# Query blocks in the order 1 to 7, 0, later turns of results, and retention weights loaded two inner blocks at a time

## The chip, the cores and the metric

The kernel runs on one core of a Trainium2 chip. The metric is device time in microseconds (us), the median of the runs shown. The engines are TensorE (PE; its weight loads are PEld), VectorE (DVE), ScalarE (ACT), GpSimd (POOL) and SyncE (SP), which here only issues DMAs.

## The reference

One layer of a decoder with three parallel branches: retention, causal pooling, and a sparse attention (NSA). It runs over a prompt of 1024 tokens and over 8 samples of 8 tokens each, with model width 1024. What the change touches is the prompt's attention and the projections of retention:

```python
z = rms_norm(x, gain) @ w_in              # 1024 -> 8984 columns, split into q, k, v, gates of all branches
o_a, s = retention(rq, rk, rv, state)     # 4 heads, chunks of 128 tokens, a 128 x 256 state a head
# attention, 8 heads in 2 groups; for every query block of 128 tokens:
o_cmp = softmax(q kc + bias) vc           # 32 compressed rows (means of 32 tokens)
o_sel = softmax(q ks + bias) vs           # all earlier tokens (16 blocks of 64 are chosen, which is all of them)
o_win = softmax(q kw + bias) vw           # the last 512 tokens
o = g0 * o_cmp + g1 * o_sel + g2 * o_win  # sigmoid gates by head
b_c = (silu(ng) * o) @ w_br_c             # likewise b_a = (silu(rg) * o_a) @ w_br_a, and b_b for pooling
y = x + (g_a * b_a + g_b * b_b + g_c * b_c) @ w_out
```

Query block i (128 tokens) reads i + 1 key blocks in the selected branch and min(i + 1, 5) in the window branch. So block 0 has one key block in each branch, and block 7 has 8 and 5.

## The kernel before

Every operand is kept as two half-precision parts (hi and lo), and a product takes three matmuls. The stages follow one another: the projections of keys, values and queries (to about 150 us of the profile), the prompt's attention (to about 496), retention (to about 740), pooling and the samples' attention (to about 880), then branch and output products. The program is written with a tile framework: its compile-time scheduler orders the instructions of each engine by modelled times and priority (earlier code first), and that order is then fixed. `issue_after(x)` and `behind()` place instructions behind a given instruction of their own engine.

*Attention.* `prompt_attention` (L719) goes through 64 heads: query blocks `order` = 0 to 7, two groups g, four heads r each. It is a pipeline over n. Step n issues the scores of head n (`head_scores`, L847: matmuls L863, L875, L884; DVE adds the bias and finds the maximum, L869 and L895), then the values of head n - 3 (LAG = 3; `head_values`, L784, matmuls L1344 to L1346 through `mm3`), then the probabilities of head n - 1 (`head_probs`, L760). The probabilities of each branch are made on ACT (L772, L773) and split into hi and lo (DVE L777, POOL L778, tile `hl`), and both parts are turned by a DMA transpose that SP issues (L780, `pt` from `hl`). `hl` and `pt` have two buffers for each branch, the score tile `S` has four.

When the four heads of a group are done (r = 3), `head_norm` (L897) scales the values by gates and sums (L903, DVE) and adds the three branches (L905 and L906, POOL) in the tile `ob`, which has one buffer. `head_out` (L909), called one step later, at r = 1 of the next group as the values lag, turns the result on PE (L913, "to") and gates it. Once a block, at n % 8 == 3, `cmp_attention` makes the compressed branch; it and `head_out` share the single PSUM buffer "tr".

*Fill.* So that PE does not stand, steps are filled with matmuls of other projections (the generator `fill`: 192 units from `silu_c` for retention's gate, then 168 from `early_gates` for the branch gates; a unit is three matmuls L319 to L321 of up to 384 columns). A head of block i brings FILL_A * (i + 1 + min(i + 1, 5)) + FILL_B = 4.0 (block 0) to 6.2 (block 7) units. 336 units go with the heads, 6 after the last head, and the last 18 in any place behind the last scores (`self.after`). Ahead of the heads stand 96 units of `silu_c` for attention's own gate.

*Weights of retention.* `load_r` (L276) loads the columns of one retention head, 8 inner blocks k of 128 x 512. Each k takes a buffer `raw` of 128 x 1024 (half used), two DMAs of 128 KB (L284, L285) and a split into `rwh` and `rwl` (`wsplit`, L230: ACT L232, DVE L233). For head 0 ACT issues the DMAs and there are two raw buffers, which the fill's weights use as well (`load_c`); for the other heads SP issues them and there are three. The retention projections (`proj_t`, L289: L298 to L300, tile z) go through k in order.

On SP, between the last transposes of attention, stand retention's constants, above all two DMAs of 512 KB for the rotary tables (`rope`, L1158).

Of the kernel before, what the change touches and what calls it, by code (L numbers as in the profile page):

```python
# [16 lines left out]
ALU = mybir.AluOpType  # L17
# [3 lines left out]
P = 128  # L21
# [17 lines left out]
LAG = 3  # L39
# [22 lines left out]
C_RET = 0  # L62
# [65 lines left out]
class Kern:  # L128
# [147 lines left out]
    def load_r(self, pool, h):  # L276

        hi, lo = [pool.tile([P, 8, 512], F16, tag="rw" + x, name=self.nm("rw" + x), bufs=1) for x in "hl"]
        w = self.d["w_in"][0]
        for k in range(8):  # L280
            raw = self.wtile([P, 1024], F32, "raw")
            r = slice(k * P, k * P + P)
            qk = w[r, C_RET:C_RET + 1024].rearrange("p (a h c) -> p a h c", a=2, c=P)[:, :, h, :]
            self.wq.dma_start(raw[:, 0:256].rearrange("p (a c) -> p a c", c=P), qk)  # L284
            self.wq.dma_start(raw[:, 256:512], w[r, 1024 + h * 256:1280 + h * 256])  # L285
            self.wsplit(hi[:, k, :], lo[:, k, :], raw[:, :512])
        return hi, lo

    def proj_t(self, out, hi, lo, t, c0, n):  # L289
# [428 lines left out]

    def prompt_attention(self, sp, ps, fill):  # L719

        order = range(8)
        heads = [(i, g, r) for i in order for g in range(2) for r in range(4)]
        sc, pr, out, oc = {}, {}, None, {}
        quota = 0.0
        for n in range(64 + LAG):
            if n < 64:
                sc[n] = self.head_scores(*heads[n], sp, ps)
            if n >= LAG:
                i, g, r = heads[n - LAG]
                if r == 0:  # L730
                    self.o = ps.tile([P, 2, 4, 64], F32, tag="o", name=self.nm("o"), bufs=A_O)
                s, nm, l = sc.pop(n - LAG)
                self.head_values(i, g, r, s, pr.pop(n - LAG), self.o, sp, ps)
                if r == 1 and out:
                    self.head_out(*out, sp, ps)
                if r == 3:
                    out = (i, g, self.head_norm(i, g, self.o, l, oc[i], sp))
            if 1 <= n <= 64:
                i, g, r = heads[n - 1]
                pr[n - 1] = self.head_probs(i, r, sc[n - 1], sp)  # L740
            if n < 64:
                i = heads[n][0]
                quota += FILL_A * (i + 1 + min(i + 1, 5)) + FILL_B
                with self.tc.issue_after(self.after.ins):
                    while quota >= 1:
                        next(fill, None)
                        quota -= 1
                if n % 8 == 3:
                    oc[i] = self.cmp_attention(i, sp, ps)
        for _ in range(6):  # L750
            next(fill, None)
        with self.tc.issue_after(self.filled.ins):
            self.head_out(*out, sp, ps)
# [140 lines left out]
    def far(self, out, in_, cf, m_in, m_out):  # L894
        self.nc.vector.tensor_scalar(out, in_, cf, m_in, op0=ALU.add, op1=ALU.max, accum_out=m_out)  # L895

    def head_norm(self, i, g, o, l, oc, sp):  # L897
        nc = self.nc
        gt = self.gate[:, i, 8:24].rearrange("p (b h) -> p b h", h=8)[:, :, 4 * g:4 * g + 4]
        self.norm_gates(l[:, 2], l[:, 0], l[:, 1], gt)  # L900
        ob = sp.tile([P, 2, 4, 64], F32, tag="ob", name=self.nm("ob"), bufs=1)
        f = l[:, 2].rearrange("p b h -> p (b h)")[:, :, None].to_broadcast([P, 8, 64])
        nc.vector.tensor_tensor(ob.rearrange("p b h c -> p (b h) c"), o.rearrange("p b h c -> p (b h) c"), f,  # L903
                                op=ALU.mult)
        nc.gpsimd.tensor_tensor(ob[:, 0], ob[:, 0], oc[:, 4 * g:4 * g + 4, :], op=ALU.add)  # L905
        nc.gpsimd.tensor_tensor(ob[:, 0], ob[:, 0], ob[:, 1], op=ALU.add)  # L906
        return ob

    def head_out(self, i, g, ob, sp, ps):  # L909
# [1074 lines left out]
```

## Time and profile before

| | |
|---|---|
| median of 3 runs | 1303.39 us (1302.78 to 1307.32) |
| the profiled execution | 1306.33 us, span 1304.5 us |
| mean granted TensorE clock | 0.986 |
| PE busy | 1251.2 us (96%) |
| PE weight loads busy | 849.4 us (65%) |
| DVE busy | 912.6 us (70%) |
| ACT busy | 630.8 us (48%) |
| POOL busy | 524.8 us (40%) |

Busy time is time in which an instruction runs on the engine; a busy PE is not PE at its peak, since the ends of its pipelined matmuls are modelled. The granted clock is the mean share of full speed that the throttle let PE have.

### The profile page before, as it was taken

Reading aid. Unit: us, or ns where it says so; the run is one execution under the profiler, and the core shown is the slowest. Engines: PE = TensorE matmul, PEld = TensorE weight load, DVE = VectorE, ACT = ScalarE, POOL = GpSimd, SP = SyncE. Lnnn points to the kernel's source line nnn. Section 1 sums busy time; section 2 is a strip of 40 time slices with the busy share of each in tenths; the row PEclk is TensorE's granted clock in tenths of the full one; section 3 lists DMA queues with packets and bytes.
Section 4 is the critical chain, followed back from the end, with each engine's and each line's share of the span. In section 5 each row is a group of like instructions: output and inputs, shape, how many; then the busy total and the mean of one; then the engine's idle time right before and its main releaser. Section 6 shows DMA issues by size and latency. Waiting matters only on the chain. (4 is left out here: it accounts for less than half of the span.)

```text
span 1304.5 us, 27790 instructions
## 1 busy us (share of the span) xinstructions
PE 1251.2 (96%) x10520; PEld 849.4 (65%) x10520; DVE 912.6 (70%) x2288; ACT 630.8 (48%) x1474; POOL 524.8 (40%) x562
## 2 busy tenths in 40 slices
PE   7999999989999989999999999999999999999995
PEld 4555666767677765555555566657788888888452
DVE  6747635788777864776766568662798877578976
ACT  5623445676666763555654444433534333212332
POOL 1112114567666751445553550101743666322124
PEclk9999999999999999999999999998999999999998
DMA  7867724598999995243741378326542121543623
GB/s 260 184 124 152 166 57 91 96 151 152 150 174 206 188 216 157 78 108 104 189 125 28 87 224 246 86 83 233 178 130 66 50 59 48 186 143 108 218 68 127
DMA packets 323419, 179.24 MB, mean 137 GB/s; under 512 B 204433, under 2 KB 297585, under 8 KB 322868
## 3 DMA queue, kind: packets, MB, share of 16 engines
q1 hardware_dynamic: 282804, 137.27, 45.3%
q10 hardware_dynamic: 35600, 26.32, 6.8%
q0 software_dynamic: 4880, 13.87, 3.3%
q8 instruction: 82, 1.34, 0.4%
q14 instruction: 53, 0.43, 0.1%
HBM read 98.80 MB, written 33.25 MB: 101 GB/s over the span
## 5 line engine op out<-in xcount | busy, mean ns | idle before, releaser
L778 POOL TENSOR_TENSOR hl<-S,hl 128x640 f16<-128x640 f32 (+7 forms) x128 | 153.9, 1211 | 122.3 <-DVE hl L777 79.5
L319 PE MATMUL pj<-xh,whi 128*128 128x384 f16 (+1 forms) x480 | 152.2, 317 | 2.4 <-ACT ue L1439 1.1
L321 PE MATMUL pj<-xh,wlo 128*128 128x384 f16 (+1 forms) x480 | 152.2, 317 | 0.0
L320 PE MATMUL pj<-xl,whi 128*128 128x384 f16 (+1 forms) x480 | 152.2, 317 | 0.0
L298 PE MATMUL z<-rwh,xh 128*128 128x512 f16 x256 | 97.7, 382 | 0.0
L300 PE MATMUL z<-rwh,xl 128*128 128x512 f16 x256 | 97.5, 381 | 0.0
L299 PE MATMUL z<-rwl,xh 128*128 128x512 f16 x256 | 97.5, 381 | 0.0
L773 ACT ACTIVATE S<-S,nm 128x640 f32<-128x640 f32 (+7 forms) x128 | 93.7, 732 | 5.4 <-DVE hst L869 1.1
L321 PEld LDWEIGHTS <-wlo 128*128 128x128 f16 x672 | 66.0, 98 | 36.5 <-issue 1.0
L320 PEld LDWEIGHTS <-whi 128*128 128x128 f16 x672 | 66.1, 98 | 36.1 <-issue 4.9
L1588 DVE TENSOR_TENSOR q<-st,q 128x288 f32<-128x288 f32 (+1 forms) x168 | 70.2, 433 | 26.4 <-PE st L1579 25.4
L319 PEld LDWEIGHTS <-whi 128*128 128x128 f16 x672 | 66.0, 98 | 33.4 <-issue 1.2
L298 PEld LDWEIGHTS <-xh 128*128 128x128 f16 x448 | 45.2, 101 | 45.7 <-issue 6.1
L232 ACT ACTIVATE whi<-raw 128x1024 f16<-128x1024 f32 (+1 forms) x48 | 45.4, 947 | 60.1 <-PE pj L320 14.7
L300 PEld LDWEIGHTS <-xl 128*128 128x128 f16 x448 | 44.1, 98 | 46.1 <-issue 2.8
L299 PEld LDWEIGHTS <-xh 128*128 128x128 f16 x448 | 44.3, 99 | 45.8 <-issue 4.8
L1344 PE MATMUL o<-vst,pt 128*128 128x64 f16 x528 | 56.7, 194 | 11.6 <-DMA pt<-hl 11.3
L772 ACT ACTIVATE hl<-S,nm 128x128 f16<-128x128 f32 (+7 forms) x64 | 49.1, 767 | 37.1 <-DMA pt<-hl 37.1
L777 DVE CAST hl<-S 128x640 f16<-128x640 f32 (+4 forms) x64 | 31.9, 498 | 50.0 <-DMA pt<-hl 18.9
L1276 POOL TENSOR_TENSOR rh<-rot,rh 128x256 f16<-128x256 f32 (+1 forms) x36 | 25.9, 720 | 90.2 <-ACT rh L1275 89.8
L320 PE MATMUL eg<-xl,whi 128*128 128x384 f16 (+1 forms) x192 | 62.1, 323 | 0.0
L321 PE MATMUL eg<-xh,wlo 128*128 128x384 f16 (+1 forms) x192 | 62.1, 323 | 0.0
(516 smaller groups left out, 4056.5 us busy)
## 6 DMA issues: line engine op xcount, KB each, us to landing
raw<-w_in SPq DMA_DIRECT2D x26, 512.0 KB
raw<-w_in ACTq DMA_DIRECT2D x18, 512.0 KB
raw<-w_in SPq DMA_DIRECT2D x48, 128.0 KB
wad<-q ACTq DMA_DIRECT2D x21, 256.0 KB
raw<-egd SPq DMA_DIRECT2D x16, 272.0 KB
s<-state_ret SPq DMA_DIRECT2D x16, 256.0 KB
o_ret_s<-s POOLq DMA_DIRECT2D x16, 256.0 KB
wr<-w_out SPq DMA_DIRECT2D x8, 512.0 KB
```

Source lines behind the costliest of these rows:

```text
L232: a = nc.scalar.activation(hi, raw, AF.Copy, scale=WS)
L298: nc.tensor.matmul(out, xh, hi[:, k, c0:c0 + n], start=(k == 0), stop=False)
L299: nc.tensor.matmul(out, xh, lo[:, k, c0:c0 + n], start=False, stop=False)
L300: self.marks["PE"] = nc.tensor.matmul(out, xl, hi[:, k, c0:c0 + n], start=False, stop=(k == 7))
L319: nc.tensor.matmul(out, hi[:, k, :], xh, start=(k == 0), stop=False)
L320: nc.tensor.matmul(out, hi[:, k, :], xl, start=False, stop=False)
L321: self.filled = nc.tensor.matmul(out, lo[:, k, :], xh, start=False, stop=(k == 7))
L772: nc.scalar.activation(hl[:, :w], s[:, d0:c1], AF.Exp, bias=nm[:, br:br + 1], scale=0.125)
L773: nc.scalar.activation(s[:, c0:c1], s[:, c0:c1], AF.Exp, bias=nm[:, br:br + 1], scale=0.125, accum_out=l[:, 0, br, r:r + 1])
L778: nc.gpsimd.tensor_tensor(hl[:, w:2 * w], s[:, d0:c1], hl[:, :w], op=ALU.subtract)
L1344: nc.tensor.matmul(out, lhs[0], rhs[0], start=start, stop=False)
L1588: nc.vector.tensor_tensor(out[:, c0:c0 + n], b, x[:, c0:c0 + n], op=ALU.add)
```

## The change

Four edits. The query blocks go in the order 1, 2, ..., 7, 0. `head_out` is called at r = 2 of the next group, one head later than before. The two additions of the very last group (n - LAG = 63) are made on DVE, all others on POOL as before. `load_r` puts two inner blocks into one `raw` buffer (four DMAs of 128 KB) and splits both with one instruction on each engine, 128 x 1024.

```diff
@@ load_r
-        for k in range(8):
+        for k2 in range(0, 8, 2):
             raw = self.wtile([P, 1024], F32, "raw")
-            r = slice(k * P, k * P + P)
-            qk = w[r, C_RET:C_RET + 1024].rearrange("p (a h c) -> p a h c", a=2, c=P)[:, :, h, :]
-            self.wq.dma_start(raw[:, 0:256].rearrange("p (a c) -> p a c", c=P), qk)
-            self.wq.dma_start(raw[:, 256:512], w[r, 1024 + h * 256:1280 + h * 256])
-            self.wsplit(hi[:, k, :], lo[:, k, :], raw[:, :512])
+            for i in range(2):
+                r = slice((k2 + i) * P, (k2 + i) * P + P)
+                qk = w[r, C_RET:C_RET + 1024].rearrange("p (a h c) -> p a h c", a=2, c=P)[:, :, h, :]
+                x = raw[:, 512 * i:512 * i + 512]
+                self.wq.dma_start(x[:, 0:256].rearrange("p (a c) -> p a c", c=P), qk)
+                self.wq.dma_start(x[:, 256:512], w[r, 1024 + h * 256:1280 + h * 256])
+            self.wsplit(*[x[:, k2:k2 + 2, :].rearrange("p k c -> p (k c)") for x in (hi, lo)], raw)
@@ prompt_attention
-        order = range(8)
+        nc = self.nc
+
+        order = (*range(1, 8), 0)
...
-                if r == 1 and out:
+                if r == 2 and out:
                     self.head_out(*out, sp, ps)
                 if r == 3:
-                    out = (i, g, self.head_norm(i, g, self.o, l, oc[i], sp))
+                    out = (i, g, self.head_norm(i, g, self.o, l, oc[i], sp, nc.vector if n - LAG == 63 else nc.gpsimd))
@@ head_norm
-    def head_norm(self, i, g, o, l, oc, sp):
+    def head_norm(self, i, g, o, l, oc, sp, eng):
...
-        nc.gpsimd.tensor_tensor(ob[:, 0], ob[:, 0], oc[:, 4 * g:4 * g + 4, :], op=ALU.add)
-        nc.gpsimd.tensor_tensor(ob[:, 0], ob[:, 0], ob[:, 1], op=ALU.add)
+        eng.tensor_tensor(ob[:, 0], ob[:, 0], oc[:, 4 * g:4 * g + 4, :], op=ALU.add)
+        eng.tensor_tensor(ob[:, 0], ob[:, 0], ob[:, 1], op=ALU.add)
```

## Rows read from the trace of the kernel before

**Rows 1.** Windows by stage: length, busy time by engine, granted clock, DMA share, GB/s.

```profile
205.00:470.00 265.00, 255.72 (x2989) 185.78 (x2987) 205.00 (x676) 184.67 (x413) 175.08 (x153) 0.99 0.89 157
470.00:497.00 27.00, 21.89 (x259) 15.08 (x258) 11.46 (x25) 12.11 (x22) 9.50 (x8) 0.94 1.05 235
```

**Rows 2.** PE's waits, 150 to 470 us: us in total, times, longest.

```profile
PE o L1344 <- DMA pt<-hl: 7.3, 11, 1.9
PE to L913 <- POOL ob L906: 1.7, 2, 1.0
```

**Rows 3.** Waits, 470 to 500 us.

```profile
PE o L1344 <- DMA pt<-hl: 4.0, 2, 3.8
```

**Rows 4.** Timeline of PE at the seam: start, us, instruction, [idle before <- releaser].

```profile
468.56 0.60 PE L863 MATMUL pn<-kst,qst 128*128 128x256 f16 x4
...
485.58 0.20 PE L1344 MATMUL o<-vst,pt 128*128 128x64 f16 x1 [3.78 <-DMA pt<-hl]
...
486.26 0.19 PE L1346 MATMUL o<-vst,pt 128*128 128x64 f16 x1
...
487.49 0.51 PE L320 MATMUL eg<-xl,whi 128*128 128x384 f16 x1
...
489.92 0.33 PE L319 MATMUL eg<-xh,whi 128*128 128x384 f16 x1
490.08 0.33 PE L320 MATMUL eg<-xl,whi 128*128 128x384 f16 x1
...
496.00 0.44 PE L913 MATMUL to<-ident,ob 128*128 128x128 f32 x2 [0.99 <-POOL ob L906]
496.28 0.38 PE L298 MATMUL z<-rwh,xh 128*128 128x512 f16 x1
...
500.81 0.38 PE L298 MATMUL z<-rwh,xh 128*128 128x512 f16 x1
```

**Rows 5.** Timeline of SP's queue at the seam.

```profile
473.13 1.12 SPq L1158 DMA_DIRECT2D rope<-c_rope  x2
...
474.36 4.47 SPq L780 DMA_TRANSPOSE pt<-hl  x1
```

**Rows 6.** Timeline of POOL at the seam.

```profile
478.27 2.14 POOL L778 TENSOR_TENSOR hl<-S,hl 128x1024 f16<-128x1024 f32 x1 [0.98 <-ACT S L773]
...
494.42 0.72 POOL L905 TENSOR_TENSOR ob<-ob,oc 128x256 f32<-128x256 f32 x1 [13.38 <-DVE ob L903]
```

**Rows 7.** Timeline of all engines in block 0, 190 to 200 us.

```profile
190.71 0.28 PE L863 MATMUL pn<-kst,qst 128*128 128x128 f16 x2
...
192.94 0.39 ACT L772 ACTIVATE hl<-S,nm 128x128 f16<-128x128 f32 x1
...
195.04 3.28 SPq L780 DMA_TRANSPOSE pt<-hl  x2
...
199.55 0.40 ACT L772 ACTIVATE hl<-S,nm 128x128 f16<-128x128 f32 x1 [2.86 <-DMA pt<-hl]
```

**Rows 8.** Timeline of DVE behind the seam.

```profile
498.95 0.68 DVE L233 SCALAR_TENSOR_TENSOR rwl<-raw,rwh 128x512 f16<-128x512 f32 x1
...
507.69 0.42 DVE L1262 TENSOR_TENSOR rot<-rot,r 128x256 f32<-128x256 f32 x1
```

**Rows 9.** Timeline of ACT and its queue at the seam.

```profile
474.46 0.42 ACTq L284 DMA_DIRECT2D raw<-w_in  x1
...
485.80 0.63 ACT L232 ACTIVATE rwh<-raw 128x512 f16<-128x512 f32 x1 [1.27 <-DMA raw<-w_in]
...
492.58 0.47 ACTq L284 DMA_DIRECT2D raw<-w_in  x1
...
498.20 0.62 ACT L232 ACTIVATE rwh<-raw 128x512 f16<-128x512 f32 x1
```

**Rows 10.** Line L232: ns min/median/max, first and last start, forms.

```profile
L232 ACT ACTIVATE rwh<-raw x32: 617/630/637, 471.1 to 638.2; 128x512 f16<-128x512 f32 x32
...
L232 ACT ACTIVATE wh<-wr x8: 1056/1057/1057, 767.1 to 805.8; 128x1024 f16<-128x1024 f32 x8
```

## The prediction

> **What bounds the kernel now.** I read the windows by stage first. TensorE (PE) is busy nearly all the time: of the 265 us of attention from 205 to 470 us it works 255.7, and DVE, ACT and POOL have 60 to 90 us to spare there [rows 1]. PE carries the span, and a change that leaves its work alone, as this one does, can win only the time in which PE stands or runs at the low clock. So I next asked for PE's waits. In the body of attention the longest sum is 7.3 us, for transposed probabilities (pt) that come by DMA; the turns of results (L913) wait 1.7 us for the sums on POOL [rows 2]. From 470 to 500 us, between the last scores and the retention projections, PE waits 4.0 us for pt [rows 3]. Third, PE's timeline there: the last scores start at 468.56, the values stand 3.78 us until 485.58, the last turn waits 0.99 us for a POOL sum, and the fill matmuls from 487.49 to 489.92 come 0.30 us apart where from 489.92 they come 0.16 apart [rows 4]; the mean granted clock of the stretch is 0.94 [rows 1], so part of it ran at the lower of the two levels. Eight matmuls in 2.43 us instead of 1.30 are 1.1 us lost. The seam thus costs 4.0 + 1.0 + 1.1 = 6.1 us.
>
> Why pt is late: SP issues the two rope loads (512 KB each) at 473.13, ahead of the last three transposes, and holds 4.47 us on the next one [rows 5]; the DMA engines move 235 GB/s there against 157 before [rows 1].
>
> **The change, part by part.** *Order 1 to 7, 0.* No instruction is added; 64 heads and 360 fill units (three matmuls each) stay. What moves is which heads drain at the seam. Block 7's heads have 39 value matmuls at 0.029 us (24 of them run from 485.58 to 486.26) [rows 4] and two large transposes; block 0's have 6 and two of 64 KB. So the 3.78 us wait and the clock fall behind it should go: -6.1 us at most, with the last edit (below) for its 1.0. In return three waits can appear.
>
> (a) Where block 7 meets block 0. The last head of block 7 needs from its scores (468.56) to the end of its subtraction on POOL (478.27 + 2.14) 11.9 us [rows 4, 6], and at least the 4.47 us of one transpose [rows 5]: 16.4. Its values come three heads later, as now, but those heads are short. The work of PE between: 6.2 + 3 x 4.0 = 18.2 fill units (FILL_A, FILL_B) x 3 x 0.16 = 8.7; values of three heads of block 7, 3 x 39 x 0.029 = 3.4; scores of three heads of block 0 at half of 0.60, 0.9: 13.0 us. The wait is 3.4 us if PE follows program order. It is nothing if the compile-time scheduler lays fill ahead of the values, as it did at the seam; above, I allow 5.0, what the seam has now [rows 3, 4], and the clock's 1.1 with it. I take 2.0.
>
> (b) The pace in block 0. A head costs PE 4.0 x 3 x 0.16 + 0.3 + 6 x 0.029 = 2.4 us. Its buffers are double: in block 0 now, one is written at 192.94 and a head's next write waits until 199.55 for a transpose to let go, 6.6 us for two heads, and SP holds 3.28 us for a head's two transposes [rows 7]. At 3.3 us a head PE would lose 0.9 x 8 = 7.2 us. But those rows are from a time in which PE ran gate matmuls between the heads and nothing pressed; the first transposes are light, and the fill can be spread. Below: nothing. I take 1.0, near the lower end.
>
> (c) The end. A head of block 0 needs from scores (190.71) to its transposes let go (199.55) 8.8 us [rows 7], then normalization and sums of about 2: 10.8. PE has 4 + 24 fill units, 28 x 3 x 0.16 = 13.4 us. That covers it, unless the rope loads stand ahead again: 1.05 MB at 235 GB/s [rows 1] are 4.5 us, and 10.8 + 4.5 - 13.4 = 1.9 us of wait. Between 0 and 1.9 I take 1.0.
>
> *Turns a head later.* Same 32 transposes, one head (2.4 to 6 us of PE) behind the sums instead of right behind the values. A sum takes POOL 0.72 us twice [rows 6], plus what is queued there, up to 2.14 us of subtraction, so a head covers it: -1.7 us [rows 2] at best, 0 at worst if other work slips into the same place. The buffer ob is single, but the next write is one head on. I take -1.5.
>
> *The last sums on DVE.* A DVE add of this shape takes 0.42 us [rows 8] against 0.72 [rows 6]: 0.6 us less in the last chain, already in the 1.0 above.
>
> *Two inner blocks at a time.* The same 64 transfers of 128 KB (two a block, L284 and L285), but one raw buffer holds two inner blocks, so twice as much is in flight, and 32 splits of 512 become 16 of 1024. ACT takes 0.63 for 512 and 1.06 for 1024 [rows 10]: 16 x (1.26 - 1.06) = 3 us less ACT time, off PE's path, so nothing. What counts is the first head's weights. Now they come in rounds: issue at 474.46, split at 485.80, 11.3 us; issue at 492.58, split at 498.20, 5.6 us [rows 9]. The last DVE half ends at 499.63 [rows 8] and PE wants that block at 500.81 [rows 4]: 1.2 us of slack, and of all splits the first is at 471.1 [rows 10], since the weights' tiles lie where attention's tables lay, which the last scores still read. With a shorter seam the old loads would be late: PE would reach the projections some 14 us after the last scores, and three rounds of 5.6 or more need 17. With pairs two are already in the raw buffers, and one round (5.6 to 11.3) with some 5 us of splits is enough: 11 to 16.5 us, wanted at 14 + 12 x 0.216 = 16.5. I count 0.3, between 0 and 1.5. So this edit earns nothing by itself; it keeps what the order wins. On SP, for the three later heads, the transposes of rotated queries (L1278) stand behind loads that wait for a raw buffer; no PE wait of that kind is in the rows, and I count nothing.
>
> The sum: -6.1 - 1.5 + 2.0 + 1.0 + 1.0 + 0.3 = -3.3 us. The profiled execution took 1306.33 us (span 1304.5): 1303.0. The median of the runs shown is 1303.39, 2.9 lower, so I forecast 1300.1.
>
> **A rule against it.** The row shows that with the rope loads and weight loads under way PE waits 4.0 us for pt [rows 3]. The Trainium skill, page "DMA: Bandwidth & Descriptors", section "Queues, rings and completion order", says that each DMA engine takes turns, packet by packet, between the queues that have work, so ACT's weight loads would share with SP's transposes whatever the order of issue. By that rule the second rival below is what happens, 1302.3 us or more; this trace fits it, but can't tell it from mere order on SP.
>
> **Rivals.** *Slower: block 0 starves PE.* At (a) 5.0 + 1.1 and at (b) up to 7.2, so that what the seam gave is paid a little earlier: -7.6 + 6.1 + 7.2 + 1.3 = +7.0, 1310. It decides as soon as (a) and (b) together pass 6.3 us. For it: two-deep buffers and 3.28 us of SP a head [rows 7]; against it: 32 fill units of block 0 that may move.
>
> *Swallowed: loads in the transposes' way.* Twice the weights in flight (512 KB more) beside block 7's transposes take 0.52 MB / 235 GB/s = 2.2 us of the DMA engines, and pt in the late blocks comes that much later, once or twice: +2.2 to +4.4 on the forecast, 1302 to 1304. For it: PE already waits 7.3 us for pt [rows 2]; against it: half of that load is there now too.
>
> *All hidden.* The scheduler covers (a) to (c) with fill: -7.6; and the 7.3 us of waits for pt [rows 2], whose places move since fill units meet other heads, shrink by up to half: -7.6 to -11.3, 1292 to 1296. For it: the scheduler did put 24 fill units among the last values. Against: it misjudged the transposes by 3.78 us there.
>
> That the turns don't move, because the scheduler places them by its own clock, is a part of the forecast (its 1.5 us) and no case of its own.
>
> **How the numbers follow.** A measurement of this kernel tells about 0.5%, 6.5 us, from no change. Chances: forecast 0.48 (its own range 1296 to 1303), all hidden 0.28, swallowed 0.14, starved 0.10. All hidden lies past -6.5, with 0.08 of the forecast: faster 0.36. Of starved, 0.07 is past +6.5: slower 0.07. Same 0.57. The range 1291.5 to 1305.5 takes in all hidden and swallowed, and leaves out most of starved and a tail below.
>
> **What the profile would show.** Right: no wait over 1 us for pt between the last scores and the first projection, and that stretch at 13 to 17 us instead of 27.7; L913 waiting under 0.3 us in all; the last retention split before PE wants it; waits of some 2 us at the first heads of block 0. Wrong: PE waits for pt of over 5 us in block 0, or for rwh or rwl at the first projection, or a new fall of the clock there. Besides, every engine's order is made anew from modelled times, and a stall in retention or later that appears or goes with that would be none of my steps.

## The result, and the profile after

The change made the kernel slower by 0.85%: 1315.99 us median of 6 runs (1311.51 to 1320.03) against 1304.51 of the kernel before on the same chip; the ratio is 1.0085, 95% interval 1.0064 to 1.0106, so some 11 us. The forecast was 1300.1. The profiled execution took 1317.53 us, span 1315.7, clock 0.983.

The windows by stage of after, beside [rows 1]:

```profile
205.00:480.00 275.00, 260.65 (x3110) 189.33 (x3109) 208.81 (x681) 186.22 (x416) 173.84 (x152) 0.99 0.86 157
480.00:505.00 25.00, 16.33 (x131) 10.94 (x129) 11.33 (x26) 12.43 (x29) 6.54 (x11) 0.85 0.69 185
```

The last scores come 11 us later than before. The second stretch is only 2 us shorter, though PE has 5.6 us less work in it: it stands 8.7 us, and the granted clock there is 0.85, not 0.94. PE's waits in after, first 150 to 480 us, beside [rows 2]:

```profile
PE o L1348 <- DMA pt<-hl: 8.3, 15, 1.9
PE tp L831 <- ACT sc L826: 3.1, 6, 1.4
PE pf L888 <- DVE S L899: 2.7, 4, 1.0
```

then 480 to 506 us, beside [rows 3]:

```profile
PE o L1348 <- DMA pt<-hl: 5.8, 4, 3.2
PE to L917 <- DVE ob L910: 2.9, 1, 2.9
```

The turns' waits of 1.7 us [rows 2] are gone. New in the body are transposes of the compressed branch (tp) that wait for ACT, and far scores (pf) that wait for a score tile from DVE. PE's timeline at the seam, beside [rows 4]:

```profile
479.69 0.39 PE L867 MATMUL pn<-kst,qst 128*128 128x128 f16 x4
...
498.19 0.24 PE L1348 MATMUL o<-vst,pt 128*128 128x64 f16 x1 [3.19 <-DMA pt<-hl]
499.36 0.23 PE L1348 MATMUL o<-vst,pt 128*128 128x64 f16 x1 [0.55 <-DMA pt<-hl]
501.43 0.24 PE L1348 MATMUL o<-vst,pt 128*128 128x64 f16 x1 [1.73 <-DMA pt<-hl]
504.62 0.66 PE L917 MATMUL to<-ident,ob 128*128 128x128 f32 x2 [2.86 <-DVE ob L910]
505.08 0.63 PE L300 MATMUL z<-rwh,xh 128*128 128x512 f16 x1
```

From 495.0 PE has no fill left, and the last values come one at a time as their transposes land, the last 21.7 us behind the last scores (501.43 - 479.69). The first projection runs at the low clock (0.63 us where [rows 4] show 0.38). What SP does meanwhile, beside [rows 5]:

```profile
487.48 1.12 SPq L1162 DMA_DIRECT2D rope<-c_rope  x2
488.99 0.55 SPq L1164 DMA_DIRECT2D rope<-c_rope  x1
489.70 0.54 SPq L1166 DMA_DIRECT2D mt<-c_mt  x1
493.83 5.67 SPq L784 DMA_TRANSPOSE pt<-hl  x4
```

The last four transposes stand behind the rope loads. What SP itself waits for before it sends them, 455 to 510 us:

```profile
SPq L784 <- POOL hl L782: 12.1, 9, 3.0
SPq L784 <- DMA rope<-c_rope: 3.5, 1, 3.5
```

The 3.5 us are a wait of SP for the landing of a rope load, which no transpose reads. The trace's records tell why: the DMAs of SP and ACT signal their landing on the same eight semaphores (counters that an engine can wait for) by turns, and this transpose has the one of the first rope load, which was sent at 487.48 and landed at 493.75; the transpose is sent at 493.83.

Who makes hl late in after, 462 to 502 us: the engines that write it wait for earlier transposes to let go of its two buffers, 8.9 us in all. The last subtraction ends at 491.66, 12.0 us behind the last scores.

```profile
ACT hl L776 <- DMA pt<-hl: 4.8, 4, 2.4
DVE hl L781 <- DMA pt<-hl: 4.1, 4, 2.1
```

```profile
491.23 0.43 POOL L782 TENSOR_TENSOR hl<-S,hl 128x128 f16<-128x128 f32 x1 [1.40 <-ACT S L777]
```

### The profile page after: what moved, and what is told of

Its sections match the earlier page's. It is cut to its first block, busy times and chain, and to the rows that moved or that the text cites. A ratio compares the mean times of both kernels' runs of the same rounds, so it can differ in the third digit from the quotient of the medians.

```text
span 1315.7 us, 27753 instructions
## 1 busy us (share of the span) xinstructions
PE 1251.1 (95%) x10520; PEld 849.8 (65%) x10520; DVE 912.9 (69%) x2274; ACT 629.2 (48%) x1458; POOL 518.8 (39%) x560
## 5 line engine op out<-in xcount | busy, mean ns | idle before, releaser
L1348 PE MATMUL o<-vst,pt 128*128 128x64 f16 x528 | 57.1, 194 | 14.3 <-DMA pt<-hl 14.1
L232 ACT ACTIVATE whi<-raw 128x1024 f16<-128x1024 f32 (+1 forms) x48 | 45.3, 946 | 51.0 <-issue 14.6
L776 ACT ACTIVATE hl<-S,nm 128x256 f16<-128x256 f32 (+7 forms) x64 | 49.1, 767 | 30.6 <-DMA pt<-hl 25.2
L233 DVE SCALAR_TENSOR_TENSOR wlo<-raw,whi 128x1024 f16<-128x1024 f32 x32 | 41.7, 1303 | 29.0 <-ACT whi L232 27.2
L1348 PEld LDWEIGHTS <-pt 128*128 128x128 f16 x528 | 47.5, 98 | 20.7 <-DMA pt<-hl 17.5
L321 PE MATMUL eg<-xh,whi 128*128 128x384 f16 (+1 forms) x192 | 60.9, 317 | 0.0
```

Source lines behind the costliest of these rows:

```text
L232: a = nc.scalar.activation(hi, raw, AF.Copy, scale=WS)
L321: nc.tensor.matmul(out, hi[:, k, :], xh, start=(k == 0), stop=False)
L776: nc.scalar.activation(hl[:, :w], s[:, d0:c1], AF.Exp, bias=nm[:, br:br + 1], scale=0.125)
L1348: nc.tensor.matmul(out, lhs[0], rhs[0], start=start, stop=False)
```

## The experiments

Three theories stood at first. A: the order costs, since block 0's short heads now drain at the end through SP, behind the rope loads. B: the paired loads cost, since more of them share the DMA engines with the transposes. C: the later turns cost by the new order that they bring to the body. Each run is timed against the kernel before on the same chip. In the table, body is from PE's first near scores (pn) to its last, seam from there to the first projection of retention; lengths and idle time (the sum of PE's waits), in us, are of one profiled execution each.

| run | ratio [95% interval] | body, idle | seam, idle | both |
|---|---|---|---|---|
| before | 1 | 318.5, 10.3 | 27.4, 5.0 | 345.9 |
| after | 1.0085 [1.0064, 1.0106] | 328.5, 14.1 | 25.2, 8.7 | 353.7 |
| order alone | 1.0052 [1.0032, 1.0072] | 326.0, 13.5 | 25.5, 9.0 | 351.5 |
| turns alone | 1.0006 [0.9988, 1.0023] | 319.4, 11.4 | 26.6, 4.4 | 346.0 |
| pairs alone | 1.0027 [1.0008, 1.0046] | 321.6, 12.8 | 27.0, 4.6 | 348.6 |
| after, constants last | 1.0033 [1.0011, 1.0054] | 330.1, 13.5 | 20.6, 4.6 | 350.7 |
| before, constants last | 0.9977 [0.9955, 0.9999] | 315.3, 9.3 | 27.0, 4.2 | 342.3 |
| order, more fill left | 1.0056 [1.0035, 1.0077] | 319.1, 16.1 | 30.6, 3.8 | 349.7 |
| block 0 seventh | 1.0089 [1.0064, 1.0113] | 326.2, 16.0 | 29.7, 6.8 | 355.9 |
| pairs, head 0 | 0.9999 [0.9982, 1.0016] | 320.5, 11.4 | 24.8, 3.7 | 345.3 |
| order, one transpose | 1.0019 [1.0005, 1.0033] | 326.3, 13.1 | 18.9, 2.3 | 345.2 |
| block 0 second | 0.9989 [0.9976, 1.0002] | 316.9, 10.7 | 28.0, 5.6 | 344.9 |
| pairs, heads 1 to 3 | 1.0011 [0.9992, 1.0031] | 319.2, 11.4 | 27.9, 5.6 | 347.1 |
| all but pairs, mended | 1.0004 [0.9990, 1.0018] | 327.0, 13.5 | 15.5, 0.9 | 342.5 |
| order, four deep | 1.0023 [1.0005, 1.0040] | 326.5, 13.4 | 15.1, 0.0 | 341.6 |
| block 0 seventh, one transpose | 1.0028 [1.0008, 1.0049] | 321.4, 12.7 | 29.1, 6.8 | 350.5 |
| after, mended | 0.9999 [0.9977, 1.0021] | 330.9, 15.0 | 15.2, 0.7 | 346.1 |
| block 0 second, constants last, turns later | 0.9984 [0.9967, 1.0000] | 315.7, 10.4 | 25.8, 3.9 | 341.5 |

One length is good to some 3 us only: "before" and "before, constants last" have the same PE instructions in the same order up to the last heads, and their bodies differ by 3.2. The ratios rest on more runs: in 32 executions before took 1298.58 to 1311.39 us. Two profiles are of long executions of their kernel: 1313.34 us of "after, mended" (median 1307.41) and 1313.37 of "block 0 second" (median 1304.59).

**One part of the change alone.** The order alone is before with `order = (*range(1, 8), 0)`.

> The kernel before with the block order 1 to 7, 0 alone. Theory A (the order costs: the eight short heads at the end drain through SP behind the rope loads, and PE waits at the seam): 1310 to 1316 us against 1304 before, with PE waits of 5 to 9 us for transposed probabilities and the last turn between the last scores and the first projection, and the clock low behind them. Theory B (the paired weight loads cost, since they share the DMA engines and the completion semaphores with the transposes): 1300 to 1305, the seam's wait gone. Theory C (the later turns cost, by a new order in the body of attention): 1300 to 1305.

It costs 0.52%, 6.8 us.

Turns alone is before with `if r == 2 and out:`.

> The kernel before with the turns of results one head later and nothing else (the last sums stay on POOL). Theory A: 1302 to 1304 us, the 1.7 us of waits for POOL sums gone in the body and nothing new. Theory B: the same. Theory C: 1308 to 1312, with new waits of the compressed branch's transposes (L827 on ACT, 3 us) and of scores for score buffers (L884 on DVE, 2.7 us) in the body, as in the changed kernel.

No change; the turns' waits for POOL fell from 2.6 us to 2.0 over body and seam. C falls.

Pairs alone has the new `load_r` and nothing else.

> The kernel before with the retention weights two inner blocks at a time and nothing else. Theory A: 1302 to 1305 us, no change, since the splits were no bound. Theory B: 1308 to 1313, with the wait of the last values (3.78 us before) grown by 2 to 5 us, and waits of the retention transposes (qt from rh) of 2 to 4 us, as in the changed kernel. Theory C: no change.

It costs 0.27%. The three add up to 0.85%, what the whole change costs: the order costs, as A has it, and the pairs do. The longer wait for the last values that B expected did not come (idle at the seam 4.6 us, 5.0 in before).

**Constants of retention behind the last transpose, in after and in before.**

```diff
+                self.last_pt = nc.sync.dma_start_transpose(t[:, :2 * w // P], hl[:, :2 * w])
...
+        with self.tc.issue_after(self.last_pt.ins):
             nc.sync.dma_start(rv, d["c_rv"])
             ... (rope, mt, mts likewise)
```

> The changed kernel with retention's constants (rotary tables, masks) queued on SP behind the last transpose of attention, everything else as changed. Theory A, as far as it blames the loads ahead of the last transposes: 5 to 8 us less than the changed kernel, 1308 to 1311 us, and no PE wait over 1 us for the last values. If the pace of the short heads alone is at fault: no change, 1316. Theory B: 0 to 3 us less. Theory C: no change, since the 5 us lost in the body stay.

In after this takes 1.0085 to 1.0033: the waits for pt at the seam fall from 5.8 to 1.3 us and its clock rises to 0.99. What stays is 3.3 us for the sums on DVE.

> The kernel before, with the constants of retention that SP loads (rv, rope, mt, mts) issued behind the last transpose of attention. If the loads ahead of the transposes cost, as the prediction read the seam: the wait of 3.78 us for pt falls under 1 us, the stretch from the last scores to the first projection shrinks from 27.4 us to 21 to 24, and the time is 4 to 6 us lower (ratio 0.995 to 0.997). Rival, rope is then late for retention or the last transposes are late by themselves: the wait moves behind the first projections or stays, ratio 0.999 to 1.001.

In before the wait did not go. PE and POOL in that run, before with the constants last:

```profile
477.71 0.23 PE L1345 MATMUL o<-vst,pt 128*128 128x64 f16 x1 [4.05 <-DMA pt<-hl]
```

```profile
471.63 2.13 POOL L778 TENSOR_TENSOR hl<-S,hl 128x1024 f16<-128x1024 f32 x1 [0.86 <-ACT S L773]
```

The subtraction ends at 473.76, and the value starts 3.95 us later with no load of SP ahead of the transpose; in before it was 485.58 - 480.41 = 5.17 [rows 4, 6]. So, by one execution of each, rope had cost 1.2 us, and the rest of the 3.78 is the last transpose's own way. The 0.23% gained here lies mostly in the body, where the order of PE is the same; I can't place it, and the interval nearly reaches 1.

**More fill left for the drain.** The order alone with `FILL_A, FILL_B = 0.2, 3.3` (3.6 before).

> The order 1 to 7, 0 alone, with FILL_B 3.3 for 3.6, so that 19 more fill units (9 us of matmuls) are left for behind the last scores. If the cost of the order is that fill runs out while block 0's last heads drain: the idle time between last scores and first projection falls from 9.0 us to under 3, body and that stretch together from 351.5 us to 345 to 347, ratio 0.999 to 1.002 against before. Rival, the body needs that fill as well: its idle time grows from 13.5 us by 4 to 8, the sum stays at 350 to 353 and the ratio at 1.004 to 1.006.

The ratio is the rival's. PE's waits for pt in this run, 150 to 467 us, against 4.8 us for the order alone:

```profile
PE o L1344 <- DMA pt<-hl: 14.7, 16, 2.7
```

At the seam no wait for pt is left, and the body pays most of it: fill that is taken from a head opens that head's wait. In all, idle time falls by 5.2 us at the seam and grows by 2.6 in the body, less than the rival said, since other waits there shrank; the ratio does not improve.

**Where block 0 stands.** `order = (*range(1, 7), 0, 7)`, and `order = (1, 0, *range(2, 8))`.

> The order 1 to 6, 0, 7, and nothing else of the change: block 7 drains at the end as before, and block 0's short heads stand in the middle. If the order costs by the drain of block 0 alone: last scores to first projection as before (27 us, 4 to 5 us of waits), body 318 to 321 us, ratio 0.999 to 1.001. Rival, block 0 costs wherever it no longer stands at the start, under the gate matmuls: body 323 to 328 us with waits for pt or for scores in and behind block 0, ratio 1.003 to 1.007.

Seventh is no cheaper than last (1.0089 against 1.0052; the intervals just overlap). So it isn't only the drain at the end: theory A falls in that form. ACT's waits in this run, 405 to 450 us, with block 0 between 409 and 430:

```profile
ACT hl L772 <- DMA pt<-hl: 5.5, 6, 1.4
```

> The order 1, 0, 2 to 7, nothing else of the change. Block 7 drains at the end as before, and block 0 is second. If block 0 is cheap only while the first gate matmuls stand beside it (they end near 205 us, before its heads would come): waits of 3 to 6 us in and behind block 0 between 205 and 250 us, ratio 1.002 to 1.006, as its place in the middle gave 1.0089. Rival, short heads cost only where long heads and their transposes are next to them (behind block 6 or 7): waits as before, ratio 0.999 to 1.001.

Second costs nothing, though the first gate matmuls end before: the expectation's first case fails. Next to short heads block 0 is free; behind long ones it is not.

**Room for four of block 0's heads.** For block 0 both branches share one tile `hl` and one tile `pt` (they are wide enough), odd and even heads take different ones, and one transpose of 128 KB turns both:

```diff
-                hl = sp.tile([...], tag=f"hl{br}", bufs=NHL)
+                b2 = br if i else r % 2
+                if i or br == 1:
+                    hb = sp.tile([...], tag=f"hl{b2}", bufs=NHL)
+                hl = hb if i or br == 1 else hb[:, 2 * P:4 * P]
...
+                if not i:
+                    nc.sync.dma_start_transpose(t[:, :4], hb[:, :4 * P])
+                    turned = [t[:, 2:4], t[:, 0:2]]
+                    continue
```

> The order 1 to 7, 0 alone, and block 0's heads put both branches into one tile hl and turn it with one transpose of 128 KB instead of two of 64, odd and even heads in different tiles, so that four heads fit where two did. If the order costs because block 0's short heads are held by their two buffers and by SP: ACT's waits for a transpose to let go of hl fall from some 12 us to under 4 in block 0, the idle time from last scores to first projection from 9.0 to 3 to 5 us, body and that stretch together from 351.5 to 345 to 348 us, ratio 0.999 to 1.003. Rival, the drain is bound by something else (loads in the DMA engines, the sums, DVE): idle time and ratio as with the order alone, 1.004 to 1.006.

1.0052 becomes 1.0019, the seam 6.6 us shorter, ACT's waits for a transpose 0.5 us where the order alone has 3.5 from 455 us on. Then the same tiles with two transposes, as before:

```diff
+                if not i:
+                    turned[br] = t[:, 2 - 2 * br:4 - 2 * br]
+                    nc.sync.dma_start_transpose(turned[br], hl[:, :2 * P])
+                    continue
```

> The order 1 to 7, 0 alone; block 0's heads take the tiles hl and pt of one branch for both branches, odd and even heads different ones, so that four heads fit, but each branch keeps its own transpose of 64 KB. If the depth of the tiles was the cause: as with one transpose, idle time before the first projection 2 to 4 us, ratio 1.000 to 1.003. Rival, the number of transposes on SP was: idle time 7 to 9 us as with the order alone, ratio 1.004 to 1.006.

1.0023, and at the seam PE doesn't wait at all. So the count of transposes was not the cause. But with the depth another thing changed. POOL, SP and a wait of SP (478 to 496 us) in the order alone:

```profile
483.49 0.43 POOL L778 TENSOR_TENSOR hl<-S,hl 128x128 f16<-128x128 f32 x1 [1.58 <-ACT S L773]
```

```profile
480.92 1.26 SPq L1158 DMA_DIRECT2D rope<-c_rope  x2
...
483.29 0.35 SPq L1162 DMA_DIRECT2D mt<-c_mt  x1
487.99 0.49 SPq L1164 DMA_DIRECT2D mts<-c_mts  x1
488.52 0.60 SPq L1172 DMA_DIRECT2D seq<-c_seq  x1
489.23 5.15 SPq L780 DMA_TRANSPOSE pt<-hl  x4
```

```profile
SPq L1164 <- DMA raw<-w_in: 4.3, 1, 4.3
```

The last subtraction ends at 483.92, and the four transposes that are then due are sent from 489.23 on, behind the constants; SP waits 4.3 us of that for one of ACT's weight loads to land before it sends mts (they signal on the same semaphore). With four deep, SP sends all transposes first (this run, beside):

```profile
477.64 8.17 SPq L786 DMA_TRANSPOSE pt<-hl  x6
485.90 0.53 SPq L1162 DMA_DIRECT2D rv<-c_rv  x1
486.48 0.98 SPq L1166 DMA_DIRECT2D rope<-c_rope  x2
```

So these runs alone can't part the depth from the place of the constants. "After, constants last" and "after, mended" below can, since the constants are behind in both: 1.0033 against 0.9999 (the intervals overlap a little), and a seam of 20.6 us against 15.2. The two stretches of "order, four deep" are 4.3 us shorter than before's, and yet it is 0.23% slower: behind the first projection it takes 813.4 us (1305.2 - 491.81), before 808.2 (1304.5 - 496.28). Only a part of that is placed: with so short a seam the weights, one inner block at a time, are late for the first projections (490 to 505 us of this run):

```profile
PE z L298 <- ACT rwh L232: 2.7, 2, 2.2
```

Block 0 seventh with the one transpose:

> The order 1 to 6, 0, 7, with block 0's two branches in one transpose and four-deep tiles. If the two-deep tiles also made the place in the middle dear (1.0089, waits of 8 us from block 0 through block 7's first heads): these waits fall to 2 to 4 us, body and stretch to the first projection together from 355.9 to 347 to 351 us, ratio 1.001 to 1.005. Rival, short heads in the middle cost by themselves: ratio 1.007 to 1.010.

1.0089 becomes 1.0028, and the body is 4.8 us shorter. The constants have no part in that, since both runs send them behind 470 us. ACT's waits of 5.5 us, 405 to 450 us, are

```profile
ACT hl L775 <- DMA pt<-hl: 1.1, 2, 0.6
```

**Whose pairs cost.** The new `load_r` for head 0 alone, and for heads 1 to 3 alone.

> Two inner blocks at a time for the weights of retention head 0 only, nothing else of the change. If the cost of the pairs (1.0027 with all four heads) lies with attention's transposes, since the first pair is loaded during block 7: body 320.5 to 322 us with waits in block 7 where before has none, no wait for qt in retention, ratio 1.001 to 1.003. Rival, the cost lies with the three later heads, whose loads SP issues ahead of qt's transposes: body 318 to 319 us, ratio 0.999 to 1.001.

> Two inner blocks at a time for the weights of retention heads 1 to 3 only. Head 0 alone gave 0.9999, all four 1.0027. If the cost lies with the later heads: retention has waits for qt of 2 to 4 us as with all four, the body of attention is as before, ratio 1.001 to 1.004. Rival, neither half costs and the 1.0027 was of the size of what moves by chance between two schedules: retention within 0.5 us of before, ratio 0.999 to 1.001.

Head 0 alone costs nothing. Of the later heads the ratio can't tell, but the profile shows a wait that before doesn't have, 500 to 750 us of that run:

```profile
PE at L1355 <- DMA qt<-rh: 4.0, 2, 2.4
```

In after it is 4.4 us. The transposes of rotated queries stand on SP behind 12 to 16 weight loads in a row, in before behind 8 at most; I take that for the cause, no run tests it.

**The whole change with both mends, and what could be kept.**

> All four edits of the change, with retention's constants on SP behind the last transpose and block 0's two branches in one transpose. If the cost of the change is made of these two and of the paired loads (0.1 to 0.3%): 1.0085 falls to 1.001 to 1.003. Rival, the pairs cost more where the stretch is short, since one round of loads is then late for the first projection: 1.004 to 1.006 with waits for rwh there.

Level with before. The seam of after with both mends, windows and then PE:

```profile
483.00:499.00 16.00, 15.27 (x124) 10.08 (x122) 9.73 (x25) 8.11 (x18) 5.53 (x8) 1.00 0.74 195
```

```profile
493.13 0.20 PE L1358 MATMUL o<-vst,pt 128*128 128x64 f16 x1 [0.33 <-DMA pt<-hl]
...
498.28 0.41 PE L926 MATMUL to<-ident,ob 128*128 128x128 f32 x2 [0.40 <-DVE ob L919]
498.52 0.38 PE L300 MATMUL z<-rwh,xh 128*128 128x512 f16 x1
```

Now the seam is what the change was to give: 15.2 us, PE busy, full clock. Yet the kernel gains nothing. In its profile the seam stands 4.3 us less than in before, and the body 4.7 us more (150 to 483 us):

```profile
PE o L1358 <- DMA pt<-hl: 9.0, 14, 2.2
PE tp L840 <- ACT sc L835: 2.9, 5, 1.4
PE pf L897 <- DVE S L908: 2.7, 4, 1.0
```

The last two come with the orders that have block 0 behind block 6 (with more fill left only tp, 1.4 us), and with block 0 first or second they are at most 0.5 us each; why these orders make ACT and DVE late there I haven't found out.

> Order 1 to 7, 0, turns a head later, last sums on VectorE, retention's constants on SP behind the last transpose, block 0's two branches in one transpose; weights one inner block at a time. If the three causes named so far (paired loads, constants ahead of the transposes, block 0 short of buffers) are all of the cost: body and the stretch to the first projection together 338 to 343 us against 345.9, ratio 0.994 to 0.999, under both kernels. Rival, the body's waits with this order remain (scores waiting for sums, the compressed branch's transposes): 346 to 350 us, ratio 1.000 to 1.003.

Also level, 1.0004, without the pairs: the rival of its expectation by the ratio, though the two stretches came out 3.4 us shorter in its profile. So in the mended kernel the pairs make no difference that can be told.

> The order 1, 0, 2 to 7, turns a head later, last sums on VectorE, retention's constants behind the last transpose, weights one inner block at a time. If the gains seen singly add (order 1, 0 first: 0.9989; constants behind: 0.9977): 0.996 to 0.998. Rival, both were chance of the size of the intervals: 0.999 to 1.001.

0.9984 [0.9967, 1.0000]. No run here is faster than before by more than 0.5%; the best are this one and before with the constants last.

## Why the prediction was wrong

**The seam, -6.1: the reading failed in its cause.** I put the wait of 3.78 us down to the rope loads ahead on SP; before with the constants last keeps 4.05 (rope's share was 1.2). That the order can clear the seam was right: with the mends it loses its waits and its low clock (13 to 17 us forecast, 15.2 measured). In the change as made it lost neither.

**(a), block 7 meeting block 0, +2.0:** 1.9 us of waits for pt in after from 455 to 480 us, the longest 1.45 in block 7's late heads. Right in size.

**(b), the pace in block 0, +1.0:** hardly there. Of the same 1.9 us only 0.2 stand within block 0's heads. Their scores come 3.3 us apart in after ((479.69 - 456.80) / 7), but as far apart with four-deep tiles (3.3 us in "order, four deep"), so it was PE's own work that set this pace, and not the buffers.

**(c), the end, +1.0: the step that failed.** (c) asked how long one head takes from its scores, 8.8 + 2 us, as if the last head had the chain to itself, and set 13.4 us of PE's work against it. In after the last turn stands 24.9 us behind the last scores (504.62 - 479.69). Where the constants are sent behind the transposes (after, constants last) it is 20.4:

```profile
482.63 0.39 PE L867 MATMUL pn<-kst,qst 128*128 128x128 f16 x4
502.98 0.66 PE L917 MATMUL to<-ident,ob 128*128 128x128 f32 x2 [3.31 <-DVE ob L910]
```

and where block 0 has four-deep tiles as well (after, mended) 15.2, with 0.40 us of wait, so that PE's own work sets it:

```profile
483.12 0.39 PE L876 MATMUL pn<-kst,qst 128*128 128x128 f16 x4
498.28 0.41 PE L926 MATMUL to<-ident,ob 128*128 128x128 f32 x2 [0.40 <-DVE ob L919]
```

So, by one profile of each, the constants cost 4.6 us of the chain, near the 4.5 that (c) named, and the queue of block 0's heads for two buffers 5.2 us, which (c) had at nothing. (After, mended also has one transpose for two; the count made no difference above.) PE had 16.5 us of work there (25.2 - 8.7), and it stood 8.7 us, with the granted clock at 0.85, where I had taken 1.0. The grounds were in the rows ("two-deep buffers and 3.28 us of SP a head"); I gave them to the rival at 0.10 and took the low end because nothing had pressed in block 0 of before.

**The rival "block 0 starves PE"** was thus right that two-deep buffers cost, but not that they set the pace in block 0. Its place was wrong (the end, not the meeting) and so was its size (1310; it came to 1316 with the constants, the clock, the body's waits and the pairs).

**The rope loads at (c), up to 1.9:** larger, since the chain they stood in was longer. SP held a transpose 3.5 us for one of them to land, and moving the constants gives back 0.5%, some 7 us with the clock, while ACT's weight loads stayed where they were. So what decided was the order in which SP sends, and a landing that it waits for. The rule of the Trainium skill that I weighed ("DMA: Bandwidth & Descriptors", section "Queues, rings and completion order", engines taking turns between queues) isn't needed for it; how much it adds to the 6.3 us that the rope load took to land, no run here shows.

**Turns a head later, -1.5:** the waits went in after, but alone the edit is worth 1.0006 [0.9988, 1.0023]: nothing.

**The last sums on DVE:** 0.42 us each, as costed. But DVE's order put a split of a weight pair ahead of them. DVE in after, beside [rows 8]:

```profile
501.86 0.69 DVE L907 TENSOR_TENSOR ob<-o,l 128x512 f32<-128x512 f32 x1 [7.66 <-issue]
502.47 1.22 DVE L233 SCALAR_TENSOR_TENSOR rwl<-raw,rwh 128x1024 f16<-128x1024 f32 x1
503.60 0.42 DVE L909 TENSOR_TENSOR ob<-ob,oc 128x256 f32<-128x256 f32 x1
```

The last turn waited 2.86 us; on POOL, in the order alone, 2.82. Nothing gained.

**Pairs, +0.3:** "earns nothing by itself; it keeps what the order wins" holds in its first half for head 0 (0.9999). The second half isn't shown: without pairs PE waits 2.7 us for rwh behind a seam of 15.1 us (order, four deep), and not at all behind one of 15.5 (all but pairs, mended). "I count nothing" for qt on SP failed: 4.4 us of waits in after, and 0.27% [0.08, 0.46] for the pairs as a whole in before, though none that can be told in the mended kernel.

**The body** was taken as unchanged but for pt. Its new 5.8 us for tp and pf no step had; they are most of what the profile still shows when all else is mended.

## What to carry to other kernels

When short work units replace long ones at a place where nothing else covers them, ask how long the last one queues for its buffers, and not only for its latency when it is alone; a tile sized for the longest unit has room for several short ones. Before a wait is charged to the load that stands ahead of a transfer, take the time from the producer's end to the consumer's start and see how much is left when the transfer has the queue to itself; and ask what the issuing engine itself waited for, which can be the landing of a load that the transfer doesn't need. And where every unit's fill just covers its chain, fill saved for the end opens waits in the middle: much of the idle time moves and doesn't go.

## What the hardware showed that I had not expected

A short wait can cost more than itself. In before a wait of 1.86 us ends at 347.97 us, and the windows behind it show the granted clock:

```profile
348.00:351.00 3.00, 2.64 (x37) 1.65 (x38) 2.51 (x9) 1.67 (x2) 1.40 (x1) 0.81 1.23 259
351.00:354.00 3.00, 3.00 (x15) 1.53 (x14) 0.84 (x1) 2.94 (x8) 2.20 (x2) 0.63 0.80 155
```

Part of each ran at the lower of the two levels: 0.19 x 3 + 0.37 x 3 = 1.7 us lost by this estimate, nearly the wait again. In the order alone a wait of 2.02 us, ended at 431.21, brought no fall (windows of that run):

```profile
431.00:434.00 3.00, 2.79 (x40) 2.19 (x40) 3.00 (x10) 1.21 (x3) 3.00 (x2) 1.00 0.85 159
434.00:437.00 3.00, 2.88 (x31) 2.12 (x30) 2.38 (x9) 1.28 (x3) 0.40 (x1) 1.00 1.23 92
```

So the length of the wait alone doesn't tell whether the clock falls.
